# A Trainium2 encoder-layer kernel: memory stored in two parts, value weights in tiles of their own, side work in another chunk order, plain cross queries, prepared SwiGLU blocks

## The chip, the core and the metric

The kernel runs on one core of one Trainium2 chip. A core has five engines that run their own instruction streams in order: TensorE (PE, matmuls), VectorE (DVE), ScalarE (ACT), GpSimd (POOL) and SyncE (SP, which here issues all the DMAs of this kernel); they wait for one another by semaphores. The metric is the device time of one execution in microseconds (us), median of several runs. Lower is better.

## The reference

One bidirectional encoder layer over two requests that share weights: 1024 and 256 tokens (1280 in all), width 1024, each request with 256 memory tokens (512 in all).

```python
def encoder_layer(x, mem, ...):
    # attention (8 differential heads) and RG-LRU in parallel, gated, one output projection
    merged = sigmoid(g_attn) * (diff_attention(q, k, v, lam) @ p_attn) \
           + sigmoid(g_lru) * ((rg_lru(conv(xr)) * gelu(yr)) @ p_lru)
    x = layer_norm(ALPHA * x + merged @ w_mix_out, ln1_g, ln1_b)
    # cross attention into the memory, 4 heads of 256
    q = (x @ xa_wq) * 256 ** -0.5
    k, v = split(mem @ xa_wkv)
    x = layer_norm(ALPHA * x + softmax(q @ k.T) @ v @ xa_wo, ln2_g, ln2_b)
    # SwiGLU, inner width 2816
    g, u = split(x @ ffn_w_in)
    return layer_norm(ALPHA * x + (silu(g) * u) @ ffn_w_out, ln3_g, ln3_b)
```

## The kernel before

**Two parts for a number.** Every fp32 operand of a large product is carried as two tiles in TensorE's fp32r type: a high part, which ACT (or DVE) copies, and a low part, which DVE or POOL subtracts (split, L180). A product is three matmuls: high by high, high by low, low by high. A weight arrives as one raw 512 KB load and is split after it (wload, L263), through two raw tiles (RW) and four tiles of parts (WT). Loads and splits have no work on TensorE; they have to be done in time.

**Stages.** Stage one (0 to 637 us) projects q, k, the LRU's inputs x and y, and last the values in two halves of 512 columns (values_out, L573): four weight tiles, then ten token tiles of 24 matmuls. Everything is stored to DRAM in two parts. Differential attention (637 to about 1372) takes pairs of 256 queries of one head: scores (L728, L729), softmax on DVE and ACT, transposes on TensorE (L754), value products (L772 to L774). Between them run the **fillers** (L663), side work that TensorE does while it would wait for a softmax: 16 memory key and value projections, then for each token chunk 16 gates and 8 LRU output projections. They are products of 24 matmuls (gemm_fm, L271; its matmuls are L278, L281, L282), all through one PSUM bank (psM), and each takes a weight of 512 KB. The chunks are `CHUNKS = ((0, 512), (512, 512), (1024, 256))`. `fill` (L700) spends them at a rate FILLT and with a priority offset FILL. What is not spent by the end of attention runs behind it. Then come the combine stage (p_attn), and the mixing projection with layer norm 1, token-major (tokmajor, L852), to about 1663.

**Cross attention** (1663 to about 1862) holds its input as seven combinations of quarters, for Strassen's seven products instead of eight (combos, L291; strassen, L347, matmuls L350 to L352 of 320 columns). The weights are combined likewise (pair_ops, L316: two raw loads, four sums L331 to L334, seven splits). The tokens are done in two segments of 640; the second segment's combinations are built at the switch from transposed tokens that were spilled to DRAM (x1t). queries (L1029) makes a head's queries, attends (L1081) its scores (L1051), softmax, transposes (L1065), and value products (L1074 to L1076). The output goes to DRAM in one part, and the output projection with layer norm 2 (tokmajor again, matmuls L874 to L876) loads and splits it.

**SwiGLU** (about 1965 to 2870) runs two halves of 640 tokens. For each of 22 blocks of inner columns, hidden (L1173) prepares the block's weights by pair_ops, does the seven products (84 matmuls of 320 columns), and out_group (L1185) adds 30 matmuls of 512 columns into the output. At the end of each half come five layer norms, and between the halves the second half's operand is combined.

**What sets the order.** A tile framework places the instructions of each engine by priority: program order, shifted where `tc.high_priority(offset=...)` stands around a piece. A tile that is asked for again waits until its last reader is done. SP issues the DMAs in one order, so a DMA that waits holds up those behind it.

## Time and profile before

| what | us |
|---|---|
| median of three runs (2874.23 to 2878.18) | 2876.78 |
| the profiled execution | 2872.01 |
| its span, from the first to the last instruction | 2870.2 |
| TensorE busy | 2743.1 (96%) |
| VectorE busy | 1848.5 (64%) |
| ScalarE busy | 1214.1 (42%) |
| GpSimd busy | 1096.2 (38%) |
| DMA | 449.09 MB, mean 156 GB/s |

The profile records one execution. "Busy" is the time in which an engine executes; TensorE's matmuls are pipelined, so the pace is read from start to start, not from the duration of one. PEclk is the clock that TensorE was granted, as a share of full speed; its mean is 0.987. A row of a timeline gives start, duration, engine, line, operation, output and inputs, shapes, and in brackets the idle time before it with what ended it.

### The profile page before, as it was taken

Reading aid. Unit: us, or ns where it says so; the run is one execution under the profiler, and the core shown is the slowest. Engines: PE = TensorE matmul, PEld = TensorE weight load, DVE = VectorE, ACT = ScalarE, POOL = GpSimd, SP = SyncE. Lnnn points to the kernel's source line nnn. Section 1 sums busy time; section 2 is a strip of 40 time slices with the busy share of each in tenths; the row PEclk is TensorE's granted clock in tenths of the full one; section 3 lists DMA queues with packets and bytes.
Section 4 is the critical chain, followed back from the end, with each engine's and each line's share of the span. In section 5 each row is a group of like instructions: output and inputs, shape, how many; then the busy total and the mean of one; then the engine's idle time right before and its main releaser. Section 6 shows DMA issues by size and latency. Waiting matters only on the chain.

```text
span 2870.2 us, 40689 instructions
## 1 busy us (share of the span) xinstructions
PE 2743.1 (96%) x15336; PEld 2423.7 (84%) x15336; DVE 1848.5 (64%) x2629; ACT 1214.1 (42%) x2067; POOL 1096.2 (38%) x709
## 2 busy tenths in 40 slices
PE   9999999988999999999799998998999997999998
PEld 7888888866888888889688897887999996899997
DVE  4446676417555565556245689787777779877776
ACT  3656445315565555557212255533223333333232
POOL 0000000005334434345301535064666669765655
PEclk9999999998999999999899999999999999999999
DMA  9333545444565575565896644645222224422221
GB/s 355 114 110 115 188 149 201 171 158 141 151 210 158 185 262 172 191 208 164 285 323 204 190 140 128 220 140 169 81 81 89 81 82 130 135 80 76 81 81 59
DMA packets 258900, 449.09 MB, mean 156 GB/s; under 512 B 19728, under 2 KB 154640, under 8 KB 258704
## 3 DMA queue, kind: packets, MB, share of 16 engines
q1 hardware_dynamic: 258704, 446.49, 47.6%
q8 instruction: 121, 1.98, 0.3%
q14 instruction: 75, 0.61, 0.1%
HBM read 316.39 MB, written 130.02 MB: 156 GB/s over the span
## 4 chain that ended last, share of the span: by engine, by line
PE 65%; DVE 15%; DMA 9%; issue 5%; ACT 4%; POOL 1%; SPq 1%; DVEq 0%; ACTq 0%; POOLq 0%
PE ps L278 4%; PE ps L282 4%; PE ps L281 4%; DMA raw<-ffn_in 3%; PE ps L515 3%; PE ps L516 3%; PE ps L517 3%; PE ps L352 3%; PE ps L350 3%; PE ps L351 3%; PE o L1193 3%; PE ps L874 3%; PE ps L876 3%; PE ps L875 3%; PE o L1194 2%
## 5 line engine op out<-in xcount | busy, mean ns | idle before, releaser
L185 POOL TENSOR_TENSOR wl<-raw,wh 128x1024 fp32r<-128x1024 f32 x132 | 320.6, 2429 | 360.8 <-ACT wh L182 237.8
L182 ACT ACTIVATE wh<-raw 128x1024 fp32r<-128x1024 f32 x204 | 215.5, 1058 | 464.9 <-PE ps L281 166.4
L352 PE MATMUL ps<-xbh,sl 128*128 128x320 f32 x976 | 302.2, 310 | 6.8 <-DVE sl L185 5.5
L350 PE MATMUL ps<-xbh,sh 128*128 128x320 f32 x976 | 302.8, 310 | 1.2 <-ACT sh L182 0.6
L351 PE MATMUL ps<-xbl,sh 128*128 128x320 f32 x976 | 301.9, 309 | 0.0
L515 PE MATMUL ps<-xh,wh 128*128 128x512 f32 (+1 forms) x768 | 273.7, 356 | 11.3 <-ACT xh L182 6.0
L278 PE MATMUL ps<-fh,wh 128*128 128x512 f32 (+1 forms) x704 | 260.1, 369 | 19.5 <-DVE g L692 16.5
L516 PE MATMUL ps<-xl,wh 128*128 128x512 f32 (+1 forms) x768 | 273.3, 356 | 0.5 <-DVE xl L185 0.5
L517 PE MATMUL ps<-xh,wl 128*128 128x512 f32 (+1 forms) x768 | 272.5, 355 | 0.5 <-DVE wl L185 0.5
L281 PE MATMUL ps<-fl,wh 128*128 128x512 f32 (+1 forms) x704 | 257.0, 365 | 0.2 <-DMA fl<-lrud 0.2
L282 PE MATMUL ps<-fh,wl 128*128 128x512 f32 (+1 forms) x704 | 256.7, 365 | 0.0
L185 POOL TENSOR_TENSOR fl<-raw,fh 128x1024 fp32r<-128x1024 f32 x4 | 9.7, 2445 | 645.6 <-DVE fh L184 633.8
L730 DVE TENSOR_REDUCE nm<-s 128x1 f32<-128x1024 f32 (+1 forms) x160 | 167.3, 1059 | 95.7 <-PE s L729 95.1
L185 DVE TENSOR_TENSOR wl<-raw,wh 128x1024 fp32r<-128x1024 f32 x116 | 169.0, 1458 | 88.3 <-ACT wh L182 87.8
L1196 DVE SCALAR_TENSOR_TENSOR y<-y,o 128x512 f32<-128x512 f32 x200 | 133.2, 681 | 101.3 <-PE o L1195 101.2
L352 PEld LDWEIGHTS ps<-xbh,sl 128*128 128x128 f32 x976 | 183.4, 188 | 11.1 <-DVE sl L185 7.1
L1193 PE MATMUL o<-wh,hh 128*128 128x512 f32 x440 | 176.0, 400 | 16.9 <-DVE y L1196 10.0
L185 POOL TENSOR_TENSOR sl<-sf,sh 128x512 fp32r<-128x512 f32 x96 | 151.7, 1582 | 101.5 <-ACT sh L182 98.9
L350 PEld LDWEIGHTS ps<-xbh,sh 128*128 128x128 f32 x976 | 183.9, 188 | 4.6 <-ACT sh L182 1.6
L351 PEld LDWEIGHTS ps<-xbl,sh 128*128 128x128 f32 x976 | 183.9, 188 | 3.6
L182 ACT ACTIVATE sh<-sf 128x512 fp32r<-128x512 f32 x192 | 118.1, 627 | 160.5 <-PE ps L351 140.6
L732 ACT ACTIVATE e<-s,nm 128x1024 f32<-128x1024 f32 (+1 forms) x160 | 158.8, 998 | 62.1 <-DVE nm L730 61.4
(278 smaller groups left out, 7646.5 us busy)
## 6 DMA issues: line engine op xcount, KB each, us to landing
raw<-ffn_in SPq DMA_DIRECT2D x88, 512.0 KB
raw<-w_in SPq DMA_DIRECT2D x80, 512.0 KB
raw<-ffn_out SPq DMA_DIRECT2D x44, 512.0 KB
q<-qd SPq DMA_DIRECT2D x320, 64.0 KB
raw<-p_lru SPq DMA_DIRECT2D x24, 512.0 KB
qd<-hl SPq DMA_DIRECT2D x16, 640.0 KB
kd<-hl SPq DMA_DIRECT2D x16, 640.0 KB
vd<-v SPq DMA_DIRECT2D x40, 256.0 KB
```

Source lines behind the costliest of these rows:

```text
L182: S.activation(h, src, AF.Copy)
L185: leng.tensor_tensor(l, src, f32(h), ALU.subtract)
L278: ins = PE.matmul(ps, a, h, start=(k == 0), stop=False)
L281: PE.matmul(ps, a, l, start=False, stop=False)
L282: PE.matmul(ps, b, h, start=False, stop=(k == 7))
L350: PE.matmul(ps, w[n][0][:, ks], xb[m][0][:, k, :], start=(k == 0), stop=False)
L351: PE.matmul(ps, w[n][0][:, ks], xb[m][1][:, k, :], start=False, stop=False)
L352: PE.matmul(ps, w[n][1][:, ks], xb[m][0][:, k, :], start=False, stop=(k == 3))
L515: PE.matmul(ps, wh[:, ks], h[:, k, :], start=(k == 0), stop=False)
L516: PE.matmul(ps, wh[:, ks], l[:, k, :], start=False, stop=False)
L517: PE.matmul(ps, wl[:, ks], h[:, k, :], start=False, stop=(k == 7))
L1193: PE.matmul(ps, hs_[a][0][:, ts], wo[a][0][:, hs], start=(a == 0), stop=False)
```

## The change

1. Stage one loads the memory at step 5, splits it and stores both parts in DRAM (memd). The side work loads them by eight DMAs instead of four raw loads and splits.
2. In values_out the second half's first three weights have a pool of their own (wv).
3. The side work takes the 256-token chunk first; FILL goes from 250 to 120, FILLT from 57 to 59.
4. Layer norm 1's transposed output is split straight into one persistent operand per chunk (x1). Cross queries are plain products, a head and a chunk at a time: per head two weights of 24 matmuls, of 512, 512 and 256 columns. The combinations and the switch of segments go. Keys and values are loaded once per head and request (8 loads of each pair of parts, before 12). Its output is stored in two parts, and the output projection loads both.
5. During cross attention the first four SwiGLU blocks are prepared: loaded, summed, split, and their 14 parts of 256 KB each stored in DRAM (fpd). In both halves hidden loads those parts (reloaded) for the first four blocks.
6. In the last block of the first half too, the output products also use the other pool's banks; in the second half, from the fourth token tile on, the last step of the layer norm is done by DVE in one pass instead of ACT and POOL in two.

```diff
-FILL = 250
-FILLT = 57.0
+FILL = 120
+FILLT = 59.0
...
+RELOAD = 4
+PREP = 100
+PREAT = {(0, 2): 0, (1, 1): 1, (2, 0): 2, (2, 2): 3}
...
         def values_out(half):
-            ws = [wload(i["w_v"][half, g], S, V) for g in range(4)]
+            ws = [wload(i["w_v"][half, g], S, V, wv if half and g < 3 else WT) for g in range(4)]
...
+            if n == 5:
+                for k in range(0, 8, 2):
+                    raw, h, l = (rot.tile([128, 2, M], d, tag=t, name="m" + t) for t, d in (("tab", F32), ("o", F32R), ("z", F32R)))
+                    SP.dma_start(raw, i["memT"][:, k:k + 2, :])
+                    split(h, l, raw, S, V)
+                    for m, z in enumerate((h, l)):
+                        SP.dma_start(memd[m, k:k + 2].rearrange("k p t -> p k t"), f32(z))
...
-            for c0, n in CHUNKS:
+            for c0, n in (CHUNKS[2], CHUNKS[0], CHUNKS[1]):
...
-            mem = fill_op(M)
-            for k in range(4):
-                raw = RW.tile([128, 2, M], F32, tag="raw", name="raw")
-                SP.dma_start(raw, i["memT"][:, 2 * k:2 * k + 2, :])
-                split(mem[0][k], mem[1][k], raw, EN[E_MH], EN[E_ML])
+            mem = stored(memd, 0, M)
...
+                h, l = x1[t // 4]
+                ts = slice(t % 4 * 128, t % 4 * 128 + 128)
                 for a in range(2):
-                    S.activation(xf[:, a * 4:a * 4 + 4, :], transposed(pt, tag, z, a), AF.Copy)
-                if t == 0:
-                    xb[:] = seven(xp)
-                if t < 5:
-                    combine1(t, xf, tp.tile([128, 4, 4, 64], F32, tag="tt", name="tt"))
-                else:
-                    SP.dma_start(x1t[:, :, (t - 5) * 128:(t - 4) * 128].rearrange("k p t -> p k t"), xf)
+                    split(h[:, a * 4:a * 4 + 4, ts], l[:, a * 4:a * 4 + 4, ts], transposed(pt, tag, z, a), S, V)
...
+            def queries(h, c):
+                if h not in qw:
+                    qw[h] = [wload(i["xa_wq"][2 * h + j], S, V) for j in range(2)]
+                q = [qp.tile([128, 2, 512], F32R, tag=t, name=t) for t in ("qh", "ql")]
+                xh, xl = x1[c]
+                n = CHUNKS[c][1]
+                for j, (wh, wl) in enumerate(qw[h]):
+                    ps = pp.tile([128, 512], F32, tag="mm", name="ps")[:, :n]
+                    for k in range(8):
+                        ks = slice(k * 128, k * 128 + 128)
+                        PE.matmul(ps, wh[:, ks], xh[:, k, :], start=(k == 0), stop=False)
+                        PE.matmul(ps, wh[:, ks], xl[:, k, :], start=False, stop=False)
+                        PE.matmul(ps, wl[:, ks], xh[:, k, :], start=False, stop=(k == 7))
+                    split(q[0][:, j, :n], q[1][:, j, :n], ps, S, V)
+                return [(*q, t * 128) for t in range(n // 128)]
...
+                ob = [ep.tile([128, 2, 256], F32R, tag="ob" + t, name="ob") for t in "hl"]
+                split(*ob, o, S, V)
+                for n in range(2):
+                    SP.dma_start(otd[n, 2 * h:2 * h + 2, :, t0:t0 + 256].rearrange("k p t -> p k t"), f32(ob[n]))
...
+            def prepare(f):
+                g = RW.tile([128, 1024], F32, tag="raw", name="raw")
+                u, sa, sb = (rx.tile([128, 1024], F32, tag="raw", name="raw") for _ in range(3))
+                SP.dma_start(g, i["ffn_in"][f])
+                SP.dma_start(u, i["ffn_in"][NF + f])
+                s1, s2, s3, s4 = sa[:, :512], sa[:, 512:], sb[:, :512], sb[:, 512:]
+                V.tensor_tensor(s1, u[:, :512], u[:, 512:], ALU.add)
+                V.tensor_tensor(s2, s1, g[:, :512], ALU.subtract)
+                V.tensor_tensor(s3, g[:, :512], u[:, :512], ALU.subtract)
+                V.tensor_tensor(s4, g[:, 512:], s2, ALU.subtract)
+                for n, src in enumerate((g[:, :512], g[:, 512:], s4, u[:, 512:], s1, s2, s3)):
+                    h, l = (op_.tile([128, 512], F32R, tag=t, name="w" + t) for t in "hl")
+                    split(h, l, src, S, V)
+                    for m, z in enumerate((h, l)):
+                        SP.dma_start(fpd[f, n, m], f32(z))
...
+            for h in range(4):
+                for c in range(3):
+                    now = h, c, queries(h, c)
+                    if (h, c) in PREAT:
+                        with tc.high_priority(offset=-PREP):
+                            prepare(PREAT[h, c])
+                    if prev is not None:
+                        attends(*prev)
+                    prev = now
...
-                split(h, l, raw, S, EN[E_OL])
+                for n, z in enumerate((h, l)):
+                    SP.dma_start(f32(z), otd[n, :, :, t * 128:t * 128 + 128].rearrange("k p t -> p k t"))
...
+            def reloaded(f):
+                if f == 0:
+                    gs = [RW.tile([128, 1024], F32, tag="raw", name="raw").bitcast(F32R) for t in "hl"]
+                else:
+                    gs = [WT.tile([128, 1024], F32R, tag="w" + t, name="w" + t) for t in "hl"]
+                u = [tuple(ws.tile([128, 512], F32R, tag=t, name="s" + t) for t in "hl") for _ in range(5)]
+                w = [tuple(g[:, c * 512:c * 512 + 512] for g in gs) for c in range(2)] + u
+                for n, _ in P_ORDER:
+                    for m in range(2):
+                        SP.dma_start(f32(w[n][m]), fpd[f, n, m])
+                return w
...
+                w = reloaded(f) if f < RELOAD else pair_ops(i["ffn_in"][f], i["ffn_in"][NF + f], [ws.tile([128, 512], F32R, tag=t, name="s" + t) for _ in range(5) for t in "hl"], rx, E_W, E_S)
...
-                        pq, tag = (pp, "mm") if last is not None and half_ and (t + half) % 4 else (po, "o")
+                        pq, tag = (pp, "mm") if last is not None and (t + half) % 4 else (po, "o")
...
-                                power = layer_norm(st, ys[t], gt, bt, end, not end)
+                                power = layer_norm(st, ys[t], gt, bt, end, not (half_ and t >= 3))
```

Three places show how instructions move. The first is SP's queue around the end of stage one, before the change. vd is the value store, fh and fl are the two parts of a side-work operand, xd the tokens, q the queries.

```order
L643 DMA fh<-xd 128x2x512 [waits DMAHW6_49]
L643 DMA fl<-xd 128x2x512 [waits DMAHW7_49]
L588 DMA vd<-v 128x512 [waits DMAHW0_49,DVE_49]
L803 DMA raw<-memT 128x1024 [waits DMAHW1_49,Pool_49]
L803 DMA raw<-memT 128x1024 [waits DMAHW2_49,Pool_49]
L265 DMA raw<-xa_wkv 128x1024 [waits DMAHW3_49,DMAHW1_49,Pool_49]
L403 DMA q<-qd 64x1x256 [waits DMAHW4_49,PE_49]
L403 DMA q<-qd 64x1x256 [waits DMAHW5_49]
L403 DMA q<-qd 64x1x256 [waits DMAHW6_49]
```

The same place after:

```order
L593 DMA vd<-v 128x512 [waits DMAHW1_49,DVE_49]
L656 DMA fh<-memd 128x2x512 [waits DMAHW2_49,PE_49]
L656 DMA fl<-memd 128x2x512 [waits DMAHW3_49,PE_49]
L656 DMA fh<-memd 128x2x512 [waits DMAHW4_49]
L656 DMA fl<-memd 128x2x512 [waits DMAHW5_49]
L656 DMA fh<-memd 128x2x512 [waits DMAHW6_49]
L656 DMA fl<-memd 128x2x512 [waits DMAHW7_49,PE_49]
L656 DMA fh<-memd 128x2x512 [waits DMAHW0_49]
L656 DMA fl<-memd 128x2x512 [waits DMAHW1_49]
L593 DMA vd<-v 128x512 [waits DMAHW2_49,Activation_49]
L593 DMA vd<-v 128x512 [waits DMAHW3_49,DVE_49]
L416 DMA vh<-vd 128x10x128 [waits DMAHW4_49,PE_49]
```

The last two raw memory loads stood behind the last value store and waited for POOL's splits; now all eight loads of both parts stand ahead of the last two value stores.

The second place is TensorE from the last value products (psv) into attention, before. s<-k,q is a score, t<-ident,e a transpose of exponentials.

```order
L728 MATMUL s<-k,q 128x512
L729 MATMUL s<-k,q 128x512
L728 MATMUL s<-k,q 128x512 [waits Activation_49]
L729 MATMUL s<-k,q 128x512
L728 MATMUL s<-k,q 128x512
L729 MATMUL s<-k,q 128x512
L754 MATMUL t<-ident,e 128x128 [waits DVE_49]
L754 MATMUL t<-ident,e 128x128 x7
L728 MATMUL s<-k,q 128x512 [waits DMAHW3_49,DMAHW7_49,PE_49,Activation_49]
```

After, where ps<-fh,wh is side work:

```order
L742 MATMUL s<-k,q 128x512
L741 MATMUL s<-k,q 128x512 [waits DMAHW2_49,DMAHW6_49,DMAHW0_49,DVE_49]
L742 MATMUL s<-k,q 128x512 [waits DMAHW6_49,DMAHW4_49]
L741 MATMUL s<-k,q 128x512
L742 MATMUL s<-k,q 128x512
L283 MATMUL ps<-fh,wh 128x512 [waits DMAHW2_49,Activation_49]
L286 MATMUL ps<-fl,wh 128x512 [waits DMAHW3_49]
L287 MATMUL ps<-fh,wl 128x512 [waits Pool_49]
L283 MATMUL ps<-fh,wh 128x512
L286 MATMUL ps<-fl,wh 128x512
```

Before, 16 score matmuls are followed by transposes, which wait for DVE; now side work stands behind the first eight score matmuls, and waits for its loads.

The third place is TensorE at the end of cross attention, before: o<-pth,vh is a value product, t<-ident,e a transpose, ps<-wh,oh the output projection.

```order
L1076 MATMUL o<-pth,vl 128x256
L1074 MATMUL o<-pth,vh 128x256
L1075 MATMUL o<-ptl,vh 128x256
L1076 MATMUL o<-pth,vl 128x256
L1065 MATMUL t<-ident,e 128x128 [waits DVE_49,PE_49]
L1065 MATMUL t<-ident,e 128x128
L1065 MATMUL t<-ident,e 128x128 [waits DVE_49]
L1065 MATMUL t<-ident,e 128x128
L874 MATMUL ps<-wh,oh 128x512
```

After, from the last value products on:

```order
L1070 MATMUL o<-pth,vl 128x256
L1068 MATMUL o<-pth,vh 128x256
L1069 MATMUL o<-ptl,vh 128x256
L1070 MATMUL o<-pth,vl 128x256
L883 MATMUL ps<-wh,oh 128x512 [waits DMAHW4_49]
L884 MATMUL ps<-wl,oh 128x512
L883 MATMUL ps<-wh,oh 128x512
L884 MATMUL ps<-wl,oh 128x512
L883 MATMUL ps<-wh,oh 128x512 [waits DMAHW5_49]
```

Before, output projection stands between the transposes and value products of the last heads; now it begins behind the last value product, and waits for loads.

## Rows read from the trace of the kernel before

**Rows 1.** Page, part 1: busy us of each engine (share of the span), instructions

```profile
PE 2743.1 (96%) x15336; PEld 2423.7 (84%) x15336; DVE 1848.5 (64%) x2629; ACT 1214.1 (42%) x2067; POOL 1096.2 (38%) x709
```

**Rows 2.** Windows: length, PE PEld DVE ACT POOL busy (count), PEclk, DMA share, GB/s

```profile
576.00:590.00 14.00, 6.62 (x25) 5.15 (x24) 2.13 (x2) 2.11 (x2) 0.00 (x0) 0.81 0.68 193
637.00:668.00 31.00, 14.85 (x50) 9.79 (x49) 18.80 (x20) 10.21 (x16) 10.69 (x6) 0.67 0.59 192
1372.00:1430.00 58.00, 39.65 (x266) 37.19 (x266) 14.36 (x24) 14.52 (x22) 16.45 (x9) 0.85 0.88 304
1663.00:1862.00 199.00, 183.93 (x1276) 175.27 (x1275) 168.90 (x282) 117.55 (x257) 65.02 (x54) 0.99 0.50 160
1962.00:2020.00 58.00, 46.76 (x279) 43.34 (x278) 46.39 (x55) 20.17 (x33) 40.72 (x23) 0.94 0.56 181
2376.00:2480.00 104.00, 85.34 (x457) 74.31 (x457) 102.00 (x119) 39.27 (x72) 99.79 (x69) 0.97 0.46 147
2490.00:2800.00 310.00, 307.58 (x1807) 284.49 (x1806) 228.37 (x301) 94.67 (x143) 185.27 (x109) 1.00 0.26 80
```

**Rows 3.** Timeline, TensorE: pairs six matmuls apart, of 512, 320 and 256 columns

```profile
569.65 0.39 PE L582 MATMUL psv<-wh,xh 128*128 128x512 f32 x1
...
571.01 0.39 PE L582 MATMUL psv<-wh,xh 128*128 128x512 f32 x1
...
1714.78 0.31 PE L350 MATMUL ps<-xbh,sh 128*128 128x320 f32 x1
...
1715.66 0.31 PE L350 MATMUL ps<-xbh,s 128*128 128x320 f32 x1
...
1716.89 0.28 PE L1074 MATMUL o<-pth,vh 128*128 128x256 f32 x1
...
1717.61 0.28 PE L1074 MATMUL o<-pth,vh 128*128 128x256 f32 x1
```

**Rows 4.** Timeline, TensorE at the switch of value halves

```profile
580.08 0.39 PE L583 MATMUL psv<-wl,xh 128*128 128x512 f32 x1
587.85 1.22 PE L582 MATMUL psv<-wh,xh 128*128 128x512 f32 x2 [7.38 <-ACT wh L182]
```

**Rows 5.** Timeline, start of attention: memory's first cast, the first transposes

```profile
649.53 0.69 DVE L184 CAST fh<-raw 128x1024 fp32r<-128x1024 f32 x1 [8.02 <-DMA raw<-memT]
...
657.13 1.97 PE L754 MATMUL t<-ident,e 128*128 128x128 f32 x8 [13.14 <-DVE e L748]
```

**Rows 6.** Windows, 20 to 40 us, the busiest DMA seen

```profile
20.00:40.00 20.00, 20.00 (x90) 16.55 (x89) 6.37 (x13) 7.84 (x11) 0.00 (x0) 1.00 1.04 376
```

**Rows 7.** Lines by form, TensorE, 1372 to 1430: busy, mean ns, idle before

```profile
L278 PE MATMUL ps<-fh,wh 128*128 128x256 f32 x72 | 23.5, 326 | 17.1 <-DVE g L692 16.2 <-DMA fh<-lrud 1.0
```

**Rows 8.** Lines by form, DVE and ACT, cross attention, 1663 to 1862

```profile
L185 DVE TENSOR_TENSOR kl<-raw,kh 128x512 fp32r<-128x512 f32 x12 | 8.8, 731 | 5.0 <-ACT kh L182 5.0
L374 DVE TENSOR_TENSOR q<-ps,q 128x320 f32<-128x320 f32 x8 | 3.8, 480 | 2.1 <-PE ps L352 2.1
L331 DVE TENSOR_TENSOR sf<-raw 128x512 f32<-128x512 f32 x7 | 5.9, 845 | 3.4 <-DMA raw<-xa_wq 3.4
...
L182 ACT ACTIVATE kh<-raw 128x512 fp32r<-128x512 f32 x12 | 7.5, 629 | 15.0 <-DMA raw<-kxd 14.0 <-issue 0.8 <-PE s L1053 0.2
```

**Rows 9.** Chain of waits, start of SwiGLU: start, us, what

```profile
1972.61 7.03 DMA raw<-ffn_in
```

**Rows 10.** Lines by form, POOL and DVE, 2355 to 2480, the halves' boundary

```profile
L185 POOL TENSOR_TENSOR sl<-sf,sh 128x512 fp32r<-128x512 f32 x11 | 18.1, 1654 | 0.0
L334 POOL TENSOR_TENSOR sf<-raw,sf 128x512 f32<-128x512 f32 x6 | 10.4, 1734 | 2.0 <-issue 1.4 <-POOL wl L185 0.7
...
L185 DVE TENSOR_TENSOR sl<-sf,sh 128x512 fp32r<-128x512 f32 x11 | 16.9, 1533 | 0.1
L331 DVE TENSOR_TENSOR sf<-raw 128x512 f32<-128x512 f32 x5 | 8.1, 1618 | 0.0
```

**Rows 11.** Timeline, DVE, the last layer norm

```profile
2862.38 3.49 DVE L849 SCALAR_TENSOR_TENSOR y<-y,rstd,lnb 128x512 f32<-128x512 f32 x2
```

More of the change, by code (lines that the diff above doesn't have):

```diff
@@ L625, in encoder_layer_kernel @@
                 kp = pool(head_pools, "kq", KB, side="right")
+                wv = pool(es, "wv", 3, side="right")
                 heads[0] = load_keys(0)
@@ L966, in encoder_layer_kernel @@
     with ExitStack() as es:
[L967 to L976 removed]
+        xp = pool(es, "xX", 1)
+        x1 = [[xp.tile([128, 8, n], F32R, tag=f"{t}{c}", name="x" + t) for t in "hl"] for c, (_, n) in enumerate(CHUNKS)]
         with ExitStack() as es1:
[L978 removed]
             def mixed(t):
@@ L1076, in attend @@
                         PE.matmul(o[:, eb, :], vl[:, m, es_], pth[:, m, :], start=False, stop=(m == 1))
-                ob = ep.tile([128, 2, 256], F32, tag="ob", name="ob")
-                S.activation(ob, o, AF.Copy)
-                SP.dma_start(otd[2 * h:2 * h + 2, :, t0:t0 + 256].rearrange("k p t -> p k t"), ob)
-            def attends(h, seg, tiles):
-                held = None
-                for n in range(len(tiles) // 2):
-                    t0 = seg * 512 + n * 256
-                    if t0 // TP != held:
-                        held = t0 // TP
-                        kv = load_kv(h, held * 256)
-                    attend(h, t0, kv, tiles[2 * n:2 * n + 2])
@@ new lines, in attends @@
+            def attends(h, c, tiles):
+                for n in range(len(tiles) // 2):
+                    t0 = CHUNKS[c][0] + n * 256
+                    if (h, t0 // TP) not in kvs:
+                        kvs[h, t0 // TP] = load_kv(h, t0 // TP * 256)
+                    attend(h, t0, kvs[h, t0 // TP], tiles[2 * n:2 * n + 2])
+            prev = None
+            for h in range(4):
[7 more added lines that the diff above has]
+                    prev = now
@@ L1238, in last @@
                                     SP.dma_start(y_out[rows, hs], ys[t][:, hs])
-                            for u in ((), (3,))[end] if t >= 3 and half_ else (t,):
+                            if not half_ or t < 3:
                                 with tc.high_priority(offset=0 if half_ else -LNP):
-                                    add = G.tensor_tensor(ys[u], ys[u], bt, ALU.add)
-                                    if end:
-                                        tc.add_manual_dep(add.ins, power.ins.name, ORDER, reason="order")
-                                    SP.dma_start(y_out[r0 + u * 128:r0 + u * 128 + 128, :], ys[u])
+                                    G.tensor_tensor(ys[t], ys[t], bt, ALU.add)
+                            if not end:
+                                with tc.high_priority(offset=0 if half_ else -LNP):
+                                    SP.dma_start(y_out[rows, :], ys[t])
                     out_group(hs_, fs, wo, ys, fs[0] == 0, last)
```

66 lines of the change are left out of this document (9 added, 57 removed).

## The prediction

> **What bounds the kernel now.** I read the engines' busy time first, then the table of stretches, then the rows inside the stretches that lose time. TensorE is busy 2743.1 us of the 2870.2 us span [rows 1], so only 127.1 us are idle, and each matmul costs its columns: six steps take 1.36 us at 512 columns, 0.88 at 320 and 0.72 at 256, that is 0.227, 0.147 and 0.120 us apiece [rows 3]. A change can therefore gain in two ways: fewer matmul columns, or less waiting. Six stretches hold the waiting [rows 2]. Their idle time is length less TensorE's busy time: 7.4, 16.2, 18.4, 15.1, 11.2 and 18.7, together 87 us of the 127. The last line of that table is a piece of steady SwiGLU with 2.4 us idle in 310: there TensorE is the bound and nothing can be had. Where the granted clock is under 1.00, matmuls are also spread out, so I count what a stretch loses by pace, not only by idleness. Value halves: 14.0 less 25 x 0.227 = 8.3 us. Attention start: 31.0 less 50 x 0.227 = 19.7 (clock 0.67). End of side work: 58.0 less 266 x 0.120 = 26. The other three have a clock near 1, so idle plus (1 - clock) x length: cross attention 15.1 + 2 = 17, start of SwiGLU 11.2 + 3.5 = 14.7, boundary of its halves 18.7 + 3.1 = 21.8. Each part of the change meets one of these six.
>
> **Value halves: gain 8.** TensorE's last matmul of half 0 starts at 580.08, the next at 587.85, waiting for ACT's split of a half 1 weight [rows 4]. That split waits for one of the four weight tiles, all held by half 0 until its end. With three tiles of their own, the first three weights are split while half 0 still runs; the fourth waits only for a tile that half 0 has finished with and has 72 matmuls of half 1's first tile in front of it. All 8.3 go, or none if the loads themselves are late: I take 8, bounds 0 and 8.3.
>
> **Attention start: gain 12.** Before, the side work cannot begin until the raw memory has landed and been split; its first cast starts at 649.53, 8.02 us idle behind the load, and TensorE sits 13.14 us until the first softmax reaches it at 657.13 [rows 5]. After, eight loads of 512 KB bring both parts ready, and TensorE's order has side work straight behind the first eight scores. The eight loads are 4.2 MB instead of 2.1; at the fastest rate that a row shows, 376 GB/s [rows 6], they take 11 us, begun about 4 us before the last value matmul. TensorE has the 8 scores and 24 side matmuls, 32 x 0.227 = 7.3 us, to put into those 7 us and the rest of the softmax wait. I leave 7 to 8 us lost, bounds 0 and 19.7 gained. The split of the memory moves into stage one, where ACT and DVE are under half busy: four pairs, of which ACT, which takes its work in order, may wait for a load: cost 1, bounds 0 and 4.
>
> **End of side work: gain 17.** Once attention is over, before has 7.5 side products of 256 columns left, each needing a 512 KB weight for 24 x 0.120 = 2.9 us of matmuls; TensorE waits 17.1 us in that row alone, nearly all of it for DVE, which empties the only PSUM bank [rows 7]. After, the 256-column chunk runs in mid attention, among attention's own matmuls, and five products of 512 columns are left: 120 x 0.227 = 27.2 us, 5.4 per weight, nearly twice the work under each load and each emptied bank. By that proportion 17.1 becomes 17.1 x 5/7.5 x 2.9/5.4 = 6; with the start of the combine stage I leave 9 of the 26. Bounds: -5 (the small products now stall TensorE inside attention, where one bank serves them too) and 26.
>
> **Cross attention: cost 6.** Certain part: 8 Strassen weight pairs x 84 matmuls of 320 columns, 672 x 0.147 = 98.8 us, become 8 weights x 24 x (0.227 + 0.227 + 0.120) = 110.2; +11.4. Against it stands the loss of 17 us. The big piece, the switch of token segments with its combinations on three engines, disappears; key and value loads fall from 12 to 8. New there: 28 splits of prepared blocks on ACT and DVE (0.63 and 0.73 each by the like rows of key parts, 17.6 and 20.4 us in all), 16 sums of 0.85, 14 us, and 20 outputs stored as two parts, where ACT's copy gains a DVE pass of 0.73, 15 us [rows 8]. DVE was busy 169 of 199 us [rows 2]; it loses 8 x 6 x 0.48 = 23 us of Strassen sums, three of the four kinds of weight sums for seven pairs, 18 us, and 14 lows that go with them, 10, so in sum it stays where it was, with fewer waits for combinations in between. Behind the last value product the order now has no output projection among the attends, which exposes the last chain of softmax. I leave 12 of the 17: net 11.4 - 5 = 6. Bounds: cost 30, gain 3.
>
> **Start of SwiGLU: gain 4.** The layer norm ahead stays. The first block waits 7.03 us for its raw weights and then for the sums and splits on DVE [rows 9]. After, the parts are loaded ready, but one block is 3.67 MB in 14 loads of 256 KB instead of 1 MB: 9.8 us at 376 GB/s. TensorE can follow as the parts come, one product (1.8 us) per 0.5 MB (1.4 us). I take 4; bounds -10 and 10.
>
> **Boundary of the halves: gain 16.** DVE is busy 102.0 and POOL 99.8 of 104 us [rows 2]: both are full, with preparing weights, combining the next half's operand and five layer norms. Preparing one block costs DVE two lows of 1.53 and three sums of about 1.6, 7.9 us, and POOL three lows of 1.65 and a sum of 1.73, 6.7 us [rows 10]. Four blocks leave the stretch: 31 and 27 us off two engines that had 2 and 4 to spare. What stays is late no longer by weights, but by the operand's combinations on POOL and DVE and by the layer norms; I leave 6 of 21.8. Bounds 0 and 21.8. The same DVE pass takes 0.731 us in cross attention, where POOL is busy 65 of 199 us [rows 2, 8], and 1.533 where POOL is full [rows 10]. The Trainium skill (GPSIMD Engine Reference, Specifications) says that GpSimd shares its SBUF interfaces with VectorE, which contend when VectorE reads two SBUF inputs. The trace agrees; by that rule what stays there gets shorter too, and the 6 would be nearer 2.
>
> **End: cost 1.** The last two normalisations are now both DVE's; the final one's two halves take 3.49 us [rows 11], and an added pass for the tile ahead of it may push them back by part of that. Bounds 0 and 3.5.
>
> **Sum.** 8 + 12 - 1 + 17 - 6 + 4 + 16 - 1 = 49 us. The profiled execution took 2872.0, so 2823; it was 4.8 below the median of the runs, 2876.8, so on that basis 2828.
>
> **Rivals.**
> A, gains half lost: everything starts as ordered, but the single PSUM bank, the in-order queues or the loads take back what the orders promise (side work in mid attention, attention start, tail of cross). For it: one bank served the side work that lost 17.1 us [rows 7]. Against: the boundary and the value halves do not depend on it. 8 + 6 - 2 + 8 - 12 + 0 + 16 - 1 = 23: 2854.
> B, the stretches close almost entirely: cross ends at -11.4 + 15 = +4, the rest at 8 + 17 + 22 + 8 + 20 = 75: 79 us, 2798.
> C, slower: prepared blocks clog cross attention. 28 pairs of stores leave through two buffers, so a buffer is refilled 13 times after its stores have landed. The place is ACT, where softmax exponentials stand behind the waiting split. It decides once a landing takes longer than the time between two uses of a buffer, with 28 pairs in some 130 us 9.3 us. The raw load of the SwiGLU start, 7.03 us [rows 9], is under that; were the stores, queued on the same engines behind other loads, twice as slow, 14.1, then 13 x 4.8 = 62 us are lost: 2890. Against it: DMA there moves 160 GB/s [rows 2], less than half of 376 [rows 6], and 14.7 MB more in 130 us is 113 GB/s.
> D, the reloads bind: the first four blocks of each half read 3.67 + 0.5 MB in a block's 84 x 0.147 + 30 x 0.227 = 19.2 us, 218 GB/s. At 376 this hides; at the 160 or so seen in cross attention it takes 26 us, 7 more for each of 8 blocks, 56 us, which would leave about 2884. The Trainium skill (DMA: Bandwidth & Descriptors, Bandwidth) asks for at least 1 MiB in a DMA to reach 75% of peak, and these are 256 KB, which speaks for D. Many in flight at once speak against it: the row at 376 [rows 6] is made of 512 KB loads.
>
> **How the numbers follow.** Forecast 0.60, near 2828, its own range 2810 to 2845. A 0.18. B 0.07. C 0.07, D 0.05. The remaining 0.03 is no net change. No change means within 0.2%, about 6 us either way, which is as much as a measurement of this kernel can tell. Faster is forecast, B and nearly all of A: 0.85; same 0.05 (the rest of A and mild C and D); slower 0.10. The range for 8 in 10 goes from B's 2798 to 2868, which takes in A and leaves C and D out.
>
> **What would show it.** Right: no pause over 2 us between the value halves; side matmuls before the first transposes; under 12 us lost after the last attention product; DVE and POOL clearly below full at the boundary of the halves; cross attention some 5 us longer. Wrong: ACT in cross attention idle for a store of a prepared block (C); TensorE waiting for reloaded parts beyond the first block (D); side matmuls waiting inside attention (A).

## The result and the profile after

The changed kernel takes 2824.9 us (median, 2822.2 to 2827.5); the kernel before takes 2877.5 in the same comparison. The ratio is 0.9818, 95% interval 0.9801 to 0.9835: 53 us faster. The profiled execution took 2822.4 us, its span 2820.5, which is 49.7 less than the span before.

The page of the changed kernel, engines' busy us (share of the span):

```profile
PE 2739.3 (97%) x15240; PEld 2411.8 (86%) x15240; DVE 1705.5 (60%) x2517; ACT 1138.6 (40%) x1921; POOL 919.3 (33%) x576
```

TensorE is 81.2 us idle instead of 127.1 [rows 1], with 11.4 us more of matmul columns. The windows of the changed kernel that answer to the first six of [rows 2], in the same order and columns. The sixth, the boundary of the halves, stands 46 us earlier than before, as the work there does:

```profile
576.00:590.00 14.00, 14.00 (x64) 11.58 (x63) 0.69 (x1) 0.60 (x1) 0.00 (x0) 1.00 0.79 197
632.00:663.00 31.00, 26.50 (x119) 20.12 (x118) 11.99 (x16) 14.11 (x21) 9.35 (x5) 1.00 0.85 286
1338.00:1396.00 58.00, 52.59 (x247) 42.54 (x246) 23.88 (x27) 17.21 (x23) 13.04 (x8) 0.97 0.86 293
1637.00:1814.00 177.00, 170.40 (x1099) 154.91 (x1098) 115.51 (x215) 90.21 (x200) 0.00 (x0) 0.98 0.70 238
1930.00:1988.00 58.00, 49.51 (x308) 47.02 (x307) 22.48 (x41) 8.33 (x13) 16.34 (x9) 0.94 0.95 340
2330.00:2434.00 104.00, 93.30 (x507) 82.61 (x506) 65.02 (x102) 24.90 (x52) 72.53 (x58) 0.97 0.73 253
```

These windows show clocks, waits and busy engines, but they do not hold exactly the same matmuls in both kernels, and the prediction read three of them by pace and three by idle time and clock. What each part of the kernel gained is read more safely from the starts of the same matmul in both: the first value product, the first score, the first matmul of the mixing projection, the last of the output projection, the 301st output product of SwiGLU, and its last. Before:

```profile
519.31 0.40 PE L582 MATMUL psv<-wh,xh 128*128 128x512 f32 x1
637.47 0.39 PE L728 MATMUL s<-k,q 128*128 128x512 f32 x1
1538.81 0.40 PE L874 MATMUL ps<-wh,oh 128*128 128x512 f32 x1
1962.20 0.39 PE L876 MATMUL ps<-wh,ol 128*128 128x512 f32 x1
2198.57 0.39 PE L1193 MATMUL o<-wh,hh 128*128 128x512 f32 x1
2858.80 0.39 PE L1195 MATMUL o<-wh,hl 128*128 128x512 f32 x1
```

and after:

```profile
522.78 0.40 PE L587 MATMUL psv<-wh,xh 128*128 128x512 f32 x1
632.78 0.39 PE L741 MATMUL s<-k,q 128*128 128x512 f32 x1
1503.98 0.40 PE L883 MATMUL ps<-wh,oh 128*128 128x512 f32 x1
1929.72 0.39 PE L885 MATMUL ps<-wh,ol 128*128 128x512 f32 x1
2161.15 0.39 PE L1202 MATMUL o<-wh,hh 128*128 128x512 f32 x1
2810.10 0.39 PE L1204 MATMUL o<-wh,hl 128*128 128x512 f32 x1
```

| stretch, from one of these starts to the next | before | after | gain | forecast |
|---|---|---|---|---|
| stage one, to the first value product | 519.3 | 522.8 | -3.5 | -1 |
| values | 118.2 | 110.0 | 8 | 8 |
| attention, its side work and the combine stage | 901.3 | 871.2 | 30 | 12 + 17 |
| mixing, cross attention and output projection | 423.4 | 425.7 | -2 | -6 |
| start of SwiGLU | 236.4 | 231.4 | 5 | 4 |
| rest of SwiGLU, with the boundary of the halves | 660.2 | 648.9 | 11 | 16 |
| end | 11.4 | 10.4 | 1 | -1 |

That is the span's 49.7 us. The 30 of attention can be divided by pace, as time less the columns of the matmuls at the pace of [rows 3]: about 15 in its first 30 us, 17 from the last score to the mixing projection, and -2 in between. The middle of attention gained nothing.

Two waits of TensorE that the change leaves, from the changed kernel's list of waits between 1800 and 2000 us (waits, total us, times, longest):

```profile
PE ps L355 <- DMA sh<-fpd: 5.8, 1, 5.8
PE o L1068 <- DVE ob L190: 5.3, 3, 2.1
```

The first is the start of SwiGLU, now waiting for the reloaded parts instead of raw weights. The second is the tail of cross attention: the output is now copied by ACT (0.59 us) and then subtracted by VectorE (0.68), and both hold its only PSUM bank, where before only the copy did.

### The profile page after: what moved, and what is told of

It is laid out like the page before. It is cut to its first block, busy times and chain, and to the rows that moved or that the text cites. A ratio compares the mean times of both kernels' runs of the same rounds, so it can differ in the third digit from the quotient of the medians.

```text
span 2820.5 us, 40319 instructions
## 1 busy us (share of the span) xinstructions
PE 2739.3 (97%) x15240; PEld 2411.8 (86%) x15240; DVE 1705.5 (60%) x2517; ACT 1138.6 (40%) x1921; POOL 919.3 (33%) x576
## 4 chain that ended last, share of the span: by engine, by line
PE 67%; DVE 11%; DMA 11%; issue 4%; ACT 4%; POOL 2%; SPq 1%; DVEq 0%; ACTq 0%; POOLq 0%
PE ps L283 4%; PE ps L286 4%; PE ps L287 4%; PE ps L357 3%; PE ps L355 3%; PE ps L356 3%; PE ps L520 3%; PE ps L521 3%; PE ps L522 3%; PE o L1202 3%; PE o L1203 3%; PE o L1204 2%; PE ps L885 2%; PE ps L883 2%; PE ps L884 2%
## 5 line engine op out<-in xcount | busy, mean ns | idle before, releaser
L187 ACT ACTIVATE wh<-raw 128x1024 fp32r<-128x1024 f32 (+1 forms) x224 | 224.4, 1006 | 492.0 <-PE ps L286 155.2
L355 PE MATMUL ps<-xbh,sh 128*128 128x320 f32 x880 | 273.1, 310 | 8.9 <-DMA sh<-fpd 7.0
L357 PE MATMUL ps<-xbh,sl 128*128 128x320 f32 x880 | 272.6, 310 | 0.4 <-DMA sl<-fpd 0.3
L356 PE MATMUL ps<-xbl,sh 128*128 128x320 f32 x880 | 272.4, 310 | 0.0
L190 DVE TENSOR_TENSOR wl<-raw,wh 128x1024 fp32r<-128x1024 f32 (+1 forms) x136 | 177.5, 1311 | 96.6 <-ACT wh L187 84.7
L850 POOL TENSOR_TENSOR rstd<-rstd,mhalf 128x1 f32<-128x1 f32 x30 | 34.5, 1152 | 498.4 <-DVE rstd L849 498.4
L355 PEld LDWEIGHTS ps<-xbh,sh 128*128 128x128 f32 x880 | 165.8, 188 | 12.8 <-DMA sh<-fpd 8.4
L520 PEld LDWEIGHTS ps<-xh,wh 128*128 128x128 f32 x768 | 146.3, 190 | 34.3 <-ACT xh L187 5.9
L1203 PE MATMUL o<-wl,hh 128*128 128x512 f32 x440 | 173.1, 394 | 0.0
L356 PEld LDWEIGHTS ps<-xbl,sh 128*128 128x128 f32 x880 | 165.9, 189 | 3.8
```

The lines of the kernel that those rows point to most:

```text
L190: leng.tensor_tensor(l, src, f32(h), ALU.subtract)
L355: PE.matmul(ps, w[n][0][:, ks], xb[m][0][:, k, :], start=(k == 0), stop=False)
L356: PE.matmul(ps, w[n][0][:, ks], xb[m][1][:, k, :], start=False, stop=False)
L357: PE.matmul(ps, w[n][1][:, ks], xb[m][0][:, k, :], start=False, stop=(k == 3))
L520: PE.matmul(ps, wh[:, ks], h[:, k, :], start=(k == 0), stop=False)
L1203: PE.matmul(ps, hs_[a][0][:, ts], wo[a][1][:, hs], start=False, stop=False)
```

## The experiments

All are made from the changed kernel, one part undone, unless said otherwise. Undone parts are compared with 2824.9 (ratio 0.9818); by the ratios the prices are up to 3 us smaller than by these medians. Where the instruction order of TensorE and SP through attention is the same (changed kernel and the last experiment), two profiled executions differ by 6 us in the time that attention takes, so a stretch of attention is not read closer than that.

**Shared tiles for the value weights** (no_wv).

```diff
-ws = [wload(i["w_v"][half, g], S, V, wv if half and g < 3 else WT) for g in range(4)]
+ws = [wload(i["w_v"][half, g], S, V) for g in range(4)]
```

> The changed kernel with the second half's value weights back in the four shared tiles. Theory (each part acts in its own stretch and the gains add): the pause between the value halves returns, the value stage is 118 us instead of 110, and the whole takes 8 us more than the changed kernel, about 2833. Rival (the gains overlap, since the eight memory loads wait for the end of stage one anyway and are late): under 3 us more, about 2827.

Measured 2846.0, ratio 0.9886 (0.9869 to 0.9904): 21 us more, not 8. Its timeline at the switch of halves, and TensorE's largest sum of waits in attention:

```profile
594.19 1.22 PE L587 MATMUL psv<-wh,xh 128*128 128x512 f32 x2 [11.44 <-ACT wh L187]
```

```profile
PE ps L283 <- DMA fh<-xd: 9.7, 3, 7.0
```

The pause is back, and longer than in [rows 4], 11.4 us for 7.4; the values take 122 us instead of 110. A second cost of 12 us, which no step of mine held, stands in attention and its end (883 us for 871, twice what like executions differ by): side work shifted later meets its operand loads (fh<-xd at a change of chunk, 9.7 us of waiting for 1.3) where attention has nothing to put in front of them. The theory that gains simply add falls, and to the other side than my rival: they lean on one another.

**Memory loaded raw** (mem_raw).

```diff
-            if n == 5:
-                ...
-            mem = stored(memd, 0, M)
+            mem = fill_op(M)
+            for k in range(4):
+                raw = RW.tile([128, 2, M], F32, tag="raw", name="raw")
+                SP.dma_start(raw, i["memT"][:, 2 * k:2 * k + 2, :])
+                split(mem[0][k], mem[1][k], raw, EN[E_MH], EN[E_ML])
```

> The changed kernel with the memory loaded raw and split at the start of attention, nothing of it in stage one. Theory: TensorE's first side product starts some 25 us into attention instead of 3, the loss up to 700 us is 24 instead of 7, and stage one gets back the 3.5 us that it lost; in all 13 to 14 us more, about 2838. Rival (the side work that starts earlier is only moved, and its share of the gain is given back behind attention): under 5 us more, about 2829.

Measured 2842.9, ratio 0.9882 (0.9863 to 0.9902): 18 us more. The window of this kernel's attention start, to be held against 26.50 busy of 31 above, and its longest wait:

```profile
626.00:657.00 31.00, 13.37 (x53) 8.96 (x52) 20.14 (x21) 11.74 (x19) 10.89 (x6) 0.78 0.56 178
```

```profile
PE t L760 <- DVE e L754: 14.9, 2, 12.0
```

The wait of [rows 5] is there again, as the theory has it. It costs more than the 13 to 14 us expected: by idle time and clock these 31 us lose 24 instead of 4.5, attention to the mixing projection takes 27 us more, and stage one gains 5 back.

**The old chunk order, the old rate and priority, both, and the priority alone.** In the four runs only these lines differ:

```diff
-FILL = 120
-FILLT = 59.0
+FILL = 250
+FILLT = 57.0
...
-            for c0, n in (CHUNKS[2], CHUNKS[0], CHUNKS[1]):
+            for c0, n in CHUNKS:
```

> The changed kernel with the side work's chunks in the order 0, 1, 2 again. Theory: the 256-token products stand behind attention again, the loss there goes from 12 to about 27 us, 13 to 16 us more in all, about 2839. Rival (the gain of that stretch came from the new FILL and FILLT, which spend the side work otherwise): under 4 us more, about 2828.

> The changed kernel with FILL 250 and FILLT 57 again, chunk order as changed. The run with the old chunk order lost nothing, and the run with the raw memory kept the short end of side work (13 us lost), so my step on the chunk order is in doubt. Theory now: the rate and the priority carry that gain; undone, the loss at the end of side work goes from 12.6 to some 25 us, 10 to 15 us more in all, about 2837. Rival (either of the two, order or rate, is enough alone): under 3 us more, about 2826.

> The changed kernel with both FILL/FILLT and the side work's chunk order as before: the fourth corner beside the changed kernel (2824.9), the old order alone (2822.2) and the old rate alone (2848.6). Loss in attention plus its end was 29.0 + 12.6 in the changed kernel, 28.8 + 8.8 with the old order, 52.6 + 12.6 with the old rate, and 25.8 + 28.9 before. Theory one (the rate brings the gain, the order costs a little at either rate): with both old the two lose about 55 us together, some 13 more than the changed kernel: about 2838. Theory two (the new order needs the new rate, and each alone is worth nothing): about 2826. Theory three (the two add as prices): 2848.6 - 2.7, about 2846.

> The changed kernel with the side work's old chunk order and the old rate FILLT 57; of the four settings of the side work only the priority offset FILL is new (120). Beside it stand the same kernel with FILLT 59 (2822.2; 28.8 lost in attention and 8.8 at its end) and with FILL 250 and FILLT 57 (2852.4; 43.1 and 25.8). Theory one (the offset carries it: side work is placed nearer to where it was made, and stands in more of attention's waits): 2821 to 2827, the two losses together under 45 us. Theory two (the rate carries it, which has the side work used up sooner): 2845 to 2853, together over 60 us. Theory three (both are needed): about 2836.

| FILL | FILLT | order | us | ratio, 95% interval |
|---|---|---|---|---|
| 120 | 59 | new (the changed kernel) | 2824.9 | 0.9818 (0.9801 to 0.9835) |
| 120 | 59 | old | 2822.2 | 0.9806 (0.9790 to 0.9821) |
| 120 | 57 | old | 2823.2 | 0.9813 (0.9797 to 0.9829) |
| 250 | 57 | new | 2848.6 | 0.9896 (0.9877 to 0.9915) |
| 250 | 57 | old | 2852.4 | 0.9910 (0.9894 to 0.9926) |

The three with FILL 120 are one time, the two with 250 another; between runs of one chunk order they are 24 and 29 us apart. The chunk order, on which my step rested, is worth nothing in the whole time that can be told at either setting, and neither is the rate at FILL 120, the only setting where it was changed alone. Attention and its end in the run with all three old:

```profile
700.00:1356.00 656.00, 638.96 (x3647) 553.58 (x3647) 383.44 (x623) 369.68 (x707) 268.46 (x162) 0.99 0.60 185
1356.00:1440.00 84.00, 68.59 (x437) 62.56 (x436) 26.43 (x43) 26.25 (x42) 24.66 (x14) 0.92 0.83 282
```

and in the run with the priority alone new:

```profile
700.00:1356.00 656.00, 651.55 (x3821) 569.57 (x3820) 383.13 (x638) 379.28 (x731) 281.40 (x170) 1.00 0.62 193
1356.00:1440.00 84.00, 76.50 (x409) 66.61 (x409) 31.88 (x49) 19.40 (x26) 11.11 (x6) 0.96 0.95 335
```

TensorE's idle time falls from 17.0 to 4.5 us in the middle of attention and from 15.4 to 7.5 at its end: a smaller offset places side products earlier among attention's instructions, where they stand in its waits. By the 257th score matmul 27 of them have started in the run with all three old and 30 in the one with the priority new. In the run with all old TensorE waits 13.9 us for the emptied PSUM bank and 5.1 for value loads, in the one with the priority 7.5, and 0.3 of the latter:

```profile
PE ps L283 <- DVE g L705: 13.9, 9, 6.4
PE o L785 <- DMA vh<-vd: 5.1, 1, 5.1
```

```profile
PE ps L283 <- DVE g L705: 7.5, 5, 4.6
```

The run with the new order and the old priority and rate (fill_250) shows what the order itself does. Its middle, its end, and two of its waits:

```profile
700.00:1338.00 638.00, 618.23 (x3654) 542.77 (x3653) 387.57 (x624) 369.95 (x711) 270.60 (x163) 0.98 0.60 185
1338.00:1440.00 102.00, 94.19 (x451) 76.78 (x450) 30.81 (x46) 27.31 (x45) 24.31 (x14) 1.00 0.79 281
```

```profile
PE ps L283 <- DMA fh<-lrud: 6.1, 3, 4.4
PE ps L283 <- DVE g L705: 5.0, 6, 0.9
```

The end is short, 7.8 us idle at full clock, as my step had it; by pace it loses 13 us less than with the old order. But attention before it loses 10 more, in waits for the side work's loads (6.1) and for softmax (4.6 and 3.9). The wait for the single PSUM bank is 5.0 us, the same as in the changed kernel, so the bank is not what takes the gain back.

**No prepared blocks; prepared blocks for the first half only; two instead of four in the second half.**

```diff
-RELOAD = 4
-PREAT = {(0, 2): 0, (1, 1): 1, (2, 0): 2, (2, 2): 3}
+RELOAD = 0
+PREAT = {}
```

```diff
-w = reloaded(f) if f < RELOAD else ...
+w = reloaded(f) if f < RELOAD and not half_ else ...
```

```diff
-w = reloaded(f) if f < RELOAD else ...
+w = reloaded(f) if f < (2 if half_ else RELOAD) else ...
```

> The changed kernel without prepared blocks: nothing of SwiGLU is prepared in cross attention, and the first four blocks of both halves are made from the raw weights as before. Theory: the boundary of the halves loses 26 us again instead of 16, the start of SwiGLU 16 instead of 11, and cross attention gains 2 to 4 us without the 28 splits and 14.7 MB of stores: 11 to 13 us more in all, about 2837. Rival one (the boundary is bound by the operand's combinations and the layer norms): the boundary loses no more than 18, in all 3 to 5 us more. Rival two (the stores are what holds cross attention back): cross attention gains 8 us or more, and the sum is within 5 us of the changed kernel.

> The changed kernel, where the prepared blocks are reloaded in the first half only and the second half makes its first four from raw weights. Theory: the start of SwiGLU keeps its gain (12 us lost), and the boundary loses 28 to 30 us as in the run without prepared blocks instead of 14, so 14 to 18 us more in all, about 2841. Rival (the boundary's gain came from the first half's blocks, which leave more time ahead of it): under 5 us more.

> The changed kernel, where the second half reloads two prepared blocks instead of four. In the changed kernel DMA runs at 342 to 394 GB/s from 2380 to 2420 us and VectorE waits there for loads. Theory (the boundary is now bound by DMA): with half the reloads there the waits for loads shrink and the 14 us lost become 10 to 14, so -4 to 0 us in all, about 2823. Rival (preparing on VectorE and GpSimd is still the dearer way): the loss goes halfway back, to 20 or more, +6 to +9 us in all, about 2833.

Measured 2843.9 (ratio 0.9879, 0.9861 to 0.9898), 2841.0 (0.9870, 0.9854 to 0.9887) and 2832.6 (0.9835, 0.9817 to 0.9854). So the prepared blocks are worth 19 us, more than the 11 to 13 expected, 16 of them in the second half, and two reloads there instead of four lose 8, as the rival has it. (The interval of that last run overlaps the changed kernel's; all four of its times are above all four of the changed kernel's, and its boundary takes 6 us more from the 481st to the 781st output product.) The boundary in the run with the first half only, its longest wait there, and the boundary in the run with two:

```profile
2330.00:2434.00 104.00, 86.29 (x467) 77.83 (x466) 92.09 (x110) 40.80 (x76) 98.48 (x72) 0.92 0.43 139
PE ps L355 <- ACT wh L187: 8.4, 1, 8.4
2330.00:2434.00 104.00, 91.17 (x488) 81.51 (x487) 77.20 (x107) 33.32 (x65) 86.12 (x67) 0.93 0.60 204
```

VectorE is busy 92.1 and 77.2 us there and GpSimd 98.5 and 86.1; in the changed kernel 65.0 and 72.5, and TensorE 93.3 instead of 86.3 and 91.2.

The wait of 8.4 us for a raw block's split was not there in the kernel before, and it shows what the 11 us of the table are. I divide the boundary at the last output product of the first half (the 660th):

| from to | before | changed | reloads in the first half only |
|---|---|---|---|
| 481st to 660th output product | 103.9 | 92.7 | 92.8 |
| 660th to 781st | 114.9 | 115.8 | 131.0 |

The run with Strassen's queries and no prepared blocks, below, has 92.6 and 130.1. So the gain of 11 us is in the last output products of the first half, with or without reloads; the only edit to SwiGLU in that run is part 6, the output products' use of the other pool's banks and the end's layer norm. With raw blocks behind it this gain is lost again at the start of the second half, and the reloads keep it. That part 6 makes it follows by exclusion: no run undoes part 6 alone.

What is late in the changed kernel is something else. Its longest wait at the boundary is for an output weight, whose cast on VectorE waits for its load:

```profile
PE o L1202 <- DVE wh L189: 4.3, 1, 4.3
L189 DVE CAST wh<-raw 128x1024 fp32r<-128x1024 f32 x4 | 4.7, 1166 | 8.2 <-DMA raw<-ffn_out 8.2
```

Two slices of it:

```profile
2380.00:2400.00 20.00, 13.01 (x69) 11.38 (x70) 10.61 (x17) 3.99 (x5) 14.90 (x8) 0.87 0.96 342
2400.00:2420.00 20.00, 18.12 (x103) 16.12 (x102) 5.65 (x11) 1.88 (x3) 6.75 (x5) 0.96 1.04 394
```

DMA is full (0.96 and 1.04, 342 and 394 GB/s), VectorE a third to half busy. I took that for the new bound, and the run with two reloads refutes it: with DMA at 0.60 instead of 0.73 of the window TensorE has less done, since two blocks are made by VectorE and GpSimd again. Both ways of getting a block cost there; reloading costs less.

**Strassen's cross queries without and with prepared blocks.** The kernel before with parts 1, 2, 3 and 6, and then with prepare and reloaded added:

```diff
+            op_ = ws
...
                         now = h, seg, queries(h, seg)
+                        if (seg, h) in PREAT:    # {(0, 2): 0, (0, 3): 1, (1, 0): 2, (1, 2): 3}
+                            with tc.high_priority(offset=-PREP):
+                                prepare(PREAT[seg, h])
```

> The kernel before with the change's parts 1, 2, 3 and 6, but Strassen's cross queries and no prepared blocks. To be compared with the run without prepared blocks (2844), from which it differs by the cross queries alone. Theory: Strassen's products have 11.4 us less of matmuls and lose about 9 us more to waiting, so it is 2 to 4 us faster than that run, about 2841. Rival (the stall at the switch of segments costs more than the matmuls save): 3 us or more slower than that run, 2847 or more.

> Strassen's cross queries as before, with the change's parts 1, 2, 3 and 6, and the four blocks prepared in cross attention, through the three tiles that the weight sums use (two tiles of their own don't fit beside Strassen's operands). Against the run with Strassen and no prepared blocks (2843.9) it gains what the reloads are worth, 18 us, if cross attention has the room. Theory (plain queries are worth nothing by themselves and pay by leaving VectorE and ScalarE room to prepare): cross attention with its projections takes 435 us or more instead of 425, and the whole is 2834 or more. Rival (the plain queries aren't needed at all): cross attention stays within 4 us, and the whole is 2824 to 2828, like the changed kernel.

Without prepared blocks: 2843.9, ratio 0.9882 (0.9863 to 0.9901), against 2843.9 for plain queries without them. The plain queries, with the key loads and the output in two parts that belong to them, are worth nothing alone: 11.4 us more of matmuls, as much less of waiting. With prepared blocks: 2881.6, ratio 1.0015 (1.0006 to 1.0025), 57 us behind the changed kernel. Its window of cross attention and ACT's splits of prepared blocks in it (count, busy, mean ns, idle before):

```profile
1655.00:1870.00 215.00, 162.17 (x1016) 153.36 (x1015) 165.27 (x274) 112.42 (x244) 58.85 (x49) 0.85 0.58 196
```

```profile
L188 ACT ACTIVATE wh<-raw 128x512 fp32r<-128x512 f32 x28 | 17.4, 628 | 22.7 <-DMA fpd<-wh 8.9 <-PE ps L357 5.5 <-issue 3.7
```

and TensorE's waits there, which name ACT's splits of query weights and keys:

```profile
PE ps L356 <- ACT s L188: 18.4, 3, 11.2
PE s L1062 <- ACT kh L188: 13.8, 5, 7.3
```

This is in part my rival C, in another kernel: ACT stands behind stores (8.9 us), and what TensorE needs stands behind ACT. But in the longest of these waits, 11.2 us from 1766 to 1777, ACT itself waits most for a raw query weight:

```profile
1774.35 0.63 ACT L188 ACTIVATE sh<-raw 128x512 fp32r<-128x512 f32 x1 [4.59 <-DMA raw<-xa_wq]
```

In the changed kernel the line of the stores reads

```profile
L187 ACT ACTIVATE wh<-raw 128x512 fp32r<-128x512 f32 x26 | 16.1, 634 | 18.7 <-DMA fpd<-wh 10.9 <-DVE wl L190 5.7 <-DVE ob L190 1.3
```

so ACT waits for stores just as much, and none of TensorE's longer waits names it. One doubt stays: this run's prepared blocks share three tiles with the weight sums, since two tiles of their own do not fit, and it has three raw tiles where the changed kernel has four. How much of the 57 us is that sharing was not separated.

**Two edits meant to gain** (banks_f0).

```diff
-PPX = 3
+PPX = 2
...
-                if f == 0:
+                if f == 0 and not half_:
                     gs = [RW.tile([128, 1024], F32, tag="raw", name="raw").bitcast(F32R) for t in "hl"]
```

> The changed kernel with two edits meant to gain. In cross attention one of three PSUM banks of the queries goes to the output (PPX 2), as TensorE waits 5.3 us there for VectorE to empty the output's only bank; expected 4 us less in the stretch of cross attention (16.3 lost there). In the second half the reloaded first block's parts go to weight tiles instead of the two raw tiles, which the next output weights need (TensorE waits 4.3 us for such a weight at the boundary, loaded late); expected 3 us less at the boundary (14.4 lost). Theory: both waits are what they seem, 2817 to 2819. Rival (DMA is full at the boundary, and the last softmax chain of cross attention is waiting for itself): less than 2 us in all, 2823 to 2825.

Measured 2838.5, ratio 0.9865 (0.9847 to 0.9884): 14 us slower. Its longest wait at the boundary, and its waits in cross attention:

```profile
2394.54 0.60 PE L355 MATMUL ps<-xbh,wh 128*128 128x320 f32 x1 [12.34 <-DMA wh<-fpd]
```

```profile
PE ps L883 <- DMA oh<-otd: 2.7, 1, 2.7
PE ps L1033 <- DVE ql L190: 2.2, 1, 2.2
```

The weight tiles are held by the first half's last output products, so the first block's parts come only behind them (the last of these products starts at 2381.8 us, the loads of these parts are issued from 2388.6): the wait of 4.3 us for an output weight is gone, and one of 12.3 for these parts stands there. In cross attention the wait for the output's bank shrank from 5.3 to 1.4 us, and the queries, with a bank less, now wait for VectorE, and the output projection for its operand. Neither theory foretold a loss. By the same matmuls these two places account for some 8 us (3 at the boundary, 5 in cross attention with its projection); the rest of the profiled execution's loss, 6, is in attention, where nothing was changed, so not all of the 14 is shown to come from the two edits. No version faster than the changed kernel beyond its interval was found; the old chunk order in it (0.9806) is as good.

## Why the prediction was right, and where not

The time, 2828 forecast and 2824.9 measured, and the sign were right: TensorE's pace bounds the kernel, and the change takes waiting out of it. A line of the trace before that bears on the first step, the split that ended the pause between the value halves:

```profile
586.74 1.06 ACT L182 ACTIVATE wh<-raw 128x1024 fp32r<-128x1024 f32 x1 [12.21 <-DMA raw<-w_v]
```

And one of the trace after that bears on the boundary, VectorE's lows of 128 x 512 from 2376 to 2480:

```profile
L190 DVE TENSOR_TENSOR sl<-sf,sh 128x512 fp32r<-128x512 f32 x4 | 3.9, 969 | 0.0
```

By the prediction's own steps:

- Value halves, gain 8: right in size and place, and the reason incomplete. It is not the weight tile alone that was late. The first two weights of half 1 were split at 570 and 571 us; the third waited for its load, which SP issued at 574.6, after those splits freed the two raw tiles, and which landed 12 us later. The pause stands some 29 matmuls into half 1 and not at its start, since 240 matmuls at 0.227 us from 519.31 end at 573.7; and three weights put 18 matmuls of a tile in front of the fourth, not 72. That undoing the part costs 21 shows what the step left out: everything behind is shifted, and side work then meets its loads elsewhere.
- Attention start, gain 12, measured about 15, and stage one 3.5 instead of 1. The mechanism was right, shown by the raw memory's return of the softmax wait; side work hid more of it than I allowed.
- End of side work, gain 17, measured about 17: the size was right by luck. The step that failed is "the 256-column chunk runs in mid attention ... nearly twice the work under each load". At the old priority the new order does make the end short, but attention before it loses 10 of the 13 us, and nothing is left that the whole time shows. At the new priority the end is short in either order. What gains is the priority offset FILL, which I listed and gave no price, and which is worth 24 to 29 us in this kernel over the whole of attention.
- Cross attention, cost 6, measured 2 with the mixing projection, with the certain 11.4 as worked out. That VectorE would stay where it was is off: it fell from 168.9 us busy of 199 to 115.5 of 177, since the lows of combined tokens and carried queries went as well, which I had not counted.
- Start of SwiGLU, gain 4, measured 5: right, and the wait is for the parts' loads.
- Boundary, gain 16, measured 11: the mis-sized term. Four blocks leaving VectorE and GpSimd free them as priced or more (102.0 to 65.0 and 99.8 to 72.5 us, for 31 and 27), and without the reloads the boundary takes 15 us more. But part 6, which had no price there, is in both kernels of that pair; against the kernel before, the whole gain is in the output products of the first half, and what remains lost is waiting for loads of reloads and output weights, not the combinations and layer norms on which "I leave 6" counted. The Trainium skill (GPSIMD Engine Reference, Specifications) speaks of interfaces shared by VectorE and GpSimd. The trace agrees: the low of 128 x 512 took 0.97 us from 2376 to 2480 with GpSimd busy 58% of the time, against 1.53 with it full [rows 10], but what it frees was no longer what TensorE waited for.
- Rival D, reloads that bind, happened there in small: TensorE waits 1.2 us for a reloaded part. The reason that the Trainium skill gave for it (DMA: Bandwidth & Descriptors, Bandwidth) did not: with 36 of 52 DMAs of 256 KB from 2376 to 2424 us and the others of 512 KB, 342 to 394 GB/s were moved, about the 376 of [rows 6]. They bind by their amount.
- Rival C's wait exists, without a price in this kernel that shows. Rival A's loss inside attention came with FILL 250 and not with FILL 120, and by other waits than the single PSUM bank's, which is 5.0 us in both.

The sum came out also because errors cancelled: the boundary 5 less than forecast and stage one 2.5 less, against 4 more in cross attention, 2 at the end, and 1 each in attention and at SwiGLU's start.

## What to carry to other kernels

When work that fills waits is placed by a priority, the priority itself is a part of the change and needs a price: here it was worth more than either part that brings the side work's loads forward. Work whose gain depends on the part behind it (part 6 at the boundary) shows no price until that part is taken away. An edit that gains nothing (plain queries for Strassen's) may still be what makes another possible, by engine time or by room for tiles, which was not separated here; only the runs with and without both show it. Undoing one part of a change measures that part with everything else in place; here four such prices (21, 18, 24 and 19 us) add to more than the whole change.

## What was not expected of the hardware

DMA held 394 GB/s over 20 us at the boundary, where most loads carry 256 KB, over the 376 of [rows 6] with 512 KB. And ACT could wait 10.9 us for stores in cross attention without a wait of TensorE that names it, while in another kernel, whose weight sums share tiles with the prepared blocks, nearly the same 8.9 us stood beside 18.4 us of TensorE's waiting for ACT, of which the longest piece had a raw load behind it.
